# First block's weights split in pieces at lower priority, first query copied by engines, three output pairs begun early

## The chip, the cores and the metric

The kernel runs on one core of one Trainium2 chip. TensorE (PE in the profile) multiplies matrices; VectorE (DVE), ScalarE (ACT) and GpSimd (POOL) work element by element beside it; SyncE (SP) issues most of the DMA transfers, in the order of its own queue. Each engine works through its own list of instructions in order, and the engines wait for one another by semaphores. The metric is the device time of one execution, in microseconds (us): the median of 3 runs of the kernel before is 2264.51 us, the lowest 2261.2 us, the highest 2265.51 us.

## The reference, cut to what matters

```
x, width 1024, 2048 tokens, fp32
h       = rmsnorm(x, g_mix)
u,q,k,v = h @ w_in                       # one combined projection, 4 x 512 columns
ya      = chunked_attention(q, k, v, rel_bias)   # 8 heads of 64; chunk of 64 sees itself and 8 before
ys      = s5_mixer(u, ...)               # diagonal complex state space, scan over tokens, GELU, GLU
x1      = x + concat(rmsnorm(ys), rmsnorm(ya)) @ w_out
out     = rmsnorm(x1 + swiglu(rmsnorm(x1)), g_final)
```

The change touches two places of this: q, k, v and the scores q·k of the first 512 tokens, and `x1` (the output projection with its residual) of the first 512 tokens. Everything is computed to fp32 accuracy.

## The kernel before, in words

**Numbers.** An fp32 value is kept as two parts, high and low, of TensorE's faster type. `split` (L151) makes them: ScalarE copies the high part, VectorE subtracts it from the value. A product is then three matmuls (`mm3`, L145): high by high, high by low, low by high. In the profile such a pair of instructions has line L153, and every matmul has line L76, every transpose L79, so the tile names tell which is which.

**Stages.** The 2048 tokens are four blocks of 512 (`SB`). The first stage makes the norm's factors and u; `att_phase` (L687) makes q, k, v, the scores and the attention, with the state-space part (`ssm_front`, `ssm_back`, whose scan runs on GpSimd) beside it; `mix_phase` (L986) gates the state-space result, norms both halves and multiplies by w_out; the two feed-forward stages follow, and they take by far the most of the time.

**Order.** The code is written against a scheduler: each instruction has a priority, by default its place in the program, and each engine's list is filled by priority among what is ready in the scheduler's own model. `tc.high_priority()` puts the instructions inside ahead of others, and with a negative offset it puts them that many places later than where they stand. TensorE's instructions are kept in program order (`keep_in_program_order`). The lists are fixed when the kernel is built: on the chip an instruction that must wait holds everything behind it on its engine.

**Attention.** There are 128 steps (block, pair of heads, head, 128 queries). In each, `scores` (L840) multiplies a piece of q with k, a VectorE instruction (L866, called ISA in the order, with result `mn`) adds the position bias and takes a minimum, ScalarE takes the exponential; later `transp` (L872) transposes and splits the result, `pv_head` multiplies by v. Projections for later steps are cut into small units and put between the steps (`Unit.advance`, L665).

**Weights of q, k and v.** There are 12 tiles of 128x1024 (0 to 3 q, 4 to 7 k, 8 to 11 v). In the first block `load_ws` (L698) loads each raw tile (two buffers `raw`, shared with x of later blocks) and splits it into one of three buffers `w`, which hold both parts; `keep_w` (L715) stores the split tile to DRAM (`wss`), from where the later blocks load it, 1 MB a tile.

**q and k of a pair.** `qk_unit` (L749) multiplies the tiles for two heads, 64 partitions each. In the first block the result `pf` is first multiplied by the norm's factors (L779: into `xt` for the first pair, `yt` for the others). For each head the high part of q goes to its 64 partitions by ScalarE (L786), the low part by VectorE (L787), and both are copied to the other 64 partitions by two DMAs on SP's queue (L788, L789), because k's high and low parts stand on the two halves of the partitions (L791, L792). For the very first pair the tiles are called `hi0x`, `lo0x` (q of head 0), `hi1x`, `lo1x` (q of head 1), `hi2x`, `lo2x` (k of heads 0 and 1); for later pairs `q2h`, `q2l`, `k`.

**Output projection.** `w_out` (L1118) is a generator for two of the eight row groups of x1, an output pair. It asks for the x tile (`xt`, two buffers), takes a PSUM tile `big` (four buffers, which together are all of PSUM), multiplies the attention half (24 matmuls), pauses, multiplies the state-space half (24 matmuls), and adds x on VectorE (L1133). The tiles `m` hold the normed halves with eight w_out tiles `woh`/`wol`. In the first block the state-space half's norm factors come late: `newton` (L97 to L110) computes them on VectorE in twelve small steps, its result is `no`, `spread` (four transposes, L79) puts them in all partitions, and `rstd2` and `mixed(b, 1)` (L1098, L153) make the tiles `m` for the state-space half. Around that the code writes the pairs by hand:

```
held = [w_out(0, b, 2 * n) for n in range(2)]
next(held[0])                          # pair 0, attention half
spread(...); rstd2(...); mixed(b, 1)
next(held[1])                          # pair 1, attention half
```

After that come the second halves of pairs 0 and 1, the sums for the next block's norms (`ones,sq`), pair 2 as a whole, the spread of those norms, and pair 3.

Of the kernel before, what the change touches and what calls it, by code (L numbers as in the profile page):

```python
# [12 lines left out]
AF = mybir.ActivationFunctionType  # L13
ALU = mybir.AluOpType
# [43 lines left out]
SB_, CB_, GB_ = 5, 5, 10  # L58
DG = 3
DGROUPS = (3, 3, 3, 2), (3, 3, 3)  # L60
LATER = 230
VO, WI, TA = range(3)
LONGS = ((VO, 0),), ((VO, 1),), ((TA, 0), (VO, 2)), ((TA, 1), (VO, 3)), ((TA, 2), (WI, 0)), ((TA, 3), (WI, 1)), ((WI, 2),), ((WI, 3),)
BLOCKS = 1, 2, 3, 0
# [29 lines left out]
def f32(ap):  # L94
    return ap.bitcast(F32)
# [55 lines left out]
def split(k, hi, lo, raw):  # L151
    nc = k.nc
    return nc.scalar.copy(hi, raw), nc.vector.tensor_tensor(lo, raw, f32(hi), op=ALU.subtract)  # L153
# [533 lines left out]
def att_phase(k, ident, S, aw, x0, roots):  # L687

    tc, nc, io, pfs = k.tc, k.nc, k.io, k.pfs
    with ExitStack() as cx:  # L690
        hT, vts, qk, keep = {0: tuple(zip(*x0))}, {}, {}, {}
# [6 lines left out]
        def load_ws(sb, ns):  # L698
            raws = [load_raw(n) for n in ns] if sb == 0 else []
            if raws and ns not in ((0, 4), (8, 10)):  # L700
                yield
            ws = []
            for i, n in enumerate(ns):
                w = k.t(aw, "w", [P, 2, 1024], F32R, bufs=WB)
                if raws:
                    for ins in split(k, w[:, 0], w[:, 1], raws[i][:]):
                        if n in (0, 4):
                            k.tc.keep_in_program_order(ins)
                    keep[n] = w
                else:  # L710
                    nc.sync.dma_start(f32(w[:]), S["ws"][n])
                ws.append((w[:, 0], w[:, 1]))
            return ws
# [34 lines left out]

        def qk_unit(sb, pr):  # L749
            ws = yield from load_ws(sb, (pr, 4 + pr))  # L750
            yield
            hi, lo = hT[sb]
            if (sb, pr) == (0, 0):
                ts = [[k.t(aw, f"{n}{q}x", [P, SB], F32R) for n, q in (("hi", hh), ("lo", hh), (("hi", "lo")[hh], 2))] for hh in range(2)]
            else:
                ts = [(k.t(aa, "q2h", [P, SB], F32R, bufs=3), k.t(aa, "q2l", [P, SB], F32R, bufs=3), k.t(aa, "k2", [P, 2 * SB], F32R, bufs=3)) for _ in range(2)]
            qk[sb, pr] = ts
            if sb > 0:
                for hh in range(2):
                    nc.sync.dma_start(f32(ts[hh][2][:, :SB]), S["k"][(sb - 1) % 2, 2 * pr + hh])  # L760
            both = (sb, pr) == (0, 0)
            pss = []
            for c in range(2):
                if c == 0 or not both:
                    cc = range(2) if both else (c,)
                    pss += [k.t(pfs, "pf", [P, 512]) for _ in cc]
                    for q in range(KT):
                        cs = slice(q * P, (q + 1) * P)
                        for m in cc:
                            wh, wl = ws[m]  # L770
                            mm3(k.ta, pss[m][:], wh[:, cs], wl[:, cs], hi[q], lo[q], q == 0, q == KT - 1)
                            if q == 2:
                                keep_w(4 * m + pr)
                        if q < KT - 1:
                            yield
                ps = pss[c]
                if sb == 0:
                    t = k.t(aa, "yt", [P, SB]) if pr else k.t(aw, "xt", [P, SB], bufs=XB)
                    nc.vector.tensor_tensor(t[:], ps[:], S["rsn"][:, :SB], op=ALU.mult)  # L779
                    ps = t  # L780
                for hh in range(2):
                    q2h, q2l, k2 = ts[hh]
                    a = slice(hh * 64, hh * 64 + 64)
                    o = slice(64 - hh * 64, 128 - hh * 64)
                    if c == 0:
                        nc.scalar.activation(q2h[a, :], ps[a, :], AF.Copy, scale=-0.125)  # L786
                        nc.vector.scalar_tensor_tensor(q2l[a, :], ps[a, :], -0.125, f32(q2h[a, :]), op0=ALU.mult, op1=ALU.subtract)  # L787
                        nc.sync.dma_start(f32(q2h[o, :]), f32(q2h[a, :]))  # L788
                        nc.sync.dma_start(f32(q2l[o, :]), f32(q2l[a, :]))  # L789
                    else:  # L790
                        nc.scalar.copy(k2[a, -SB:], ps[a, :])  # L791
                        nc.vector.tensor_tensor(k2[o, -SB:], ps[a, :], f32(k2[a, -SB:]), op=ALU.subtract)  # L792
                        if sb < NSB - 1:
                            nc.sync.dma_start(S["k"][sb % 2, 2 * pr + hh], f32(k2[:, -SB:]))
                yield
# [190 lines left out]
def mix_phase(k, S, bank):  # L986

    tc, nc, io = k.tc, k.nc, k.io
    te = k.te
    with ExitStack() as cx:  # L990
# [109 lines left out]
        def big():  # L1100
            return k.t(psum, *BIG)
# [16 lines left out]
        def w_out(sb, b, i):  # L1118
            ts = slice(sb * SB, (sb + 1) * SB)
            if i == 0:  # L1120
                b.sa = k.t(k.mf, "sa", [P, SB], bufs=2)
            rows = slice(i * P, (i + 2) * P)
            xt = k.t(wr, "xt", [P, 1024], bufs=2)
            xv = xt[:].rearrange("p (q t) -> p q t", q=2)
            nc.sync.dma_start(xv, io["xt"][rows, ts].rearrange("(q p) t -> p q t", p=P))
            ps = k.t(psum, *BIG)
            for n, c in ((n, c) for m in range(2) for c in range(2) for n in range(4 * m, 4 * m + 4)):
                if n == 4 and c == 0:
                    yield
                fc = slice((i + c) * P, (i + c + 1) * P)  # L1130
                for q in QS[n : n + 1]:
                    mm3(te, ps[:, c * 512 : (c + 1) * 512], W[q][0][:, fc], W[q][1][:, fc], b.m[q][0], b.m[q][1], n == 0, n == 7)
            nc.vector.tensor_tensor(xt[:], xt[:], ps[:], op=ALU.add)  # L1133
            nc.sync.dma_start(S["x1"][rows, ts].rearrange("(q p) t -> p q t", p=P), xv)
            if i == 0:
                nc.scalar.activation(b.sa[:], xt[:, :512], AF.Square)
                nc.scalar.activation(xt[:, 512:], xt[:, 512:], AF.Square)
            else:
                nc.scalar.activation(xt[:], xt[:], AF.Square)
                nc.vector.tensor_tensor(b.sa[:], b.sa[:], xt[:, :512], op=ALU.add)  # L1140
            nc.vector.tensor_tensor(b.sa[:], b.sa[:], xt[:, 512:], op=ALU.add)
            yield
# [22 lines left out]
        b = load(0, True)  # L1165
        load_a(b, 0)
        raws = [load_wo(n, wr, "xt") for n in range(2)]
# [30 lines left out]
        for sb in range(NSB):  # L1198
            if sb:
                b.m = {}  # L1200
                mixed(b, 0)
            if sb == 0:
                held = [w_out(0, b, 2 * n) for n in range(2)]
                next(held[0])
                ps = big()
                spread(k, te, ps[:, :512], b.o[1], 0)
                with tc.high_priority():
                    rstd2(b, 1, ps[:, :512])
                    mixed(b, 1)
                next(held[1])  # L1210
            else:
                mixed(b, 1)
            for n in range(4):
                if n == 0 and 0 < sb < NSB - 1:
                    nxt = next_block(sb + 1)
                if sb or n > 1:
                    for _ in w_out(sb, b, 2 * n):
                        pass
                else:
                    next(held[n])  # L1220
                if n in (0, 1) and xr:
                    next(xr)
                if n in (1, 2) and sb + 1 < NSB:
                    norm(nxt, n - 1)
                for _ in range(PRE0.get((sb, n), 0)):
                    next(pre)
                if (sb, n) == (NSB - 1, 1):
                    rx.close()
                    k.ga1 = tc.alloc_tile_pool(name="ga1", reuse_waits="tile", bufs=1, side="right")
                    k.gr = tc.alloc_tile_pool(name="gr", reuse_waits="tile", bufs=2, side="right")  # L1230
                    wr = cx.enter_context(tc.tile_pool(name="wr2", reuse_waits="tile", bufs=2, side="right"))
                    k.hT = build(k, S, 0, k.ga1, EARLY)
            if sb < NSB - 1:
                xr = rstd_steps(k, te, psum, k.mf, BIG, b.sa[:], D, S["rsn"][:, sb * SB : (sb + 1) * SB])
            if sb == 1:
                pre = pre_steps(k, S, 0, pre_tiles().__next__, True)
            k.last = b.sa[:]
            b = nxt
# [498 lines left out]
```

## Time and profile before

| what | value |
|---|---|
| median of 3 runs (lowest to highest) | 2264.51 us (2261.2 to 2265.51) |
| profiled execution, its own time | 2267.91 us |
| span of the profiled execution | 2266.1 us |
| mean granted TensorE clock | 0.982 |
| TensorE busy | 2165.6 us, 96% |
| VectorE busy | 1542.4 us, 68% |
| ScalarE busy | 1003.3 us, 44% |
| GpSimd busy | 351.2 us, 15% |

The span runs from the first to the last instruction, and the profiled execution's own time is 1.8 us longer. "Busy" counts matmuls with modelled ends, so a busy TensorE is not one that runs at full speed; the granted clock tells the speed. The rows of the timeline give start, duration, engine, line, operation, output<-inputs by the program's names, and in brackets the time for which the engine stood idle before and what it waited for. A row with "x2" groups instructions that follow each other.

### The profile page before, as it was taken

Reading aid. Unit: us, or ns where it says so; the run is one execution under the profiler, and the core shown is the slowest. Engines: PE = TensorE matmul, PEld = TensorE weight load, DVE = VectorE, ACT = ScalarE, POOL = GpSimd, SP = SyncE. Lnnn points to the kernel's source line nnn. Section 1 sums busy time; section 2 is a strip of 40 time slices with the busy share of each in tenths; the row PEclk is TensorE's granted clock in tenths of the full one; section 3 lists DMA queues with packets and bytes.
Section 4 is the critical chain, followed back from the end, with each engine's and each line's share of the span. In section 5 each row is a group of like instructions: output and inputs, shape, how many; then the busy total and the mean of one; then the engine's idle time right before and its main releaser. Section 6 shows DMA issues by size and latency. Waiting matters only on the chain.

```text
span 2266.1 us, 30134 instructions
## 1 busy us (share of the span) xinstructions
PE 2165.6 (96%) x10632; PEld 1825.8 (81%) x10632; DVE 1542.4 (68%) x2695; ACT 1003.3 (44%) x1656; POOL 351.2 (15%) x827
## 2 busy tenths in 40 slices
PE   8988899999997899999999999999999999999997
PEld 6777788898986788778888887888888778888886
DVE  7756666556557756776766668766656477688776
ACT  5445555556557442353333335333333443353322
POOL 2246576656500000000000000000000010000000
PEclk9999999999998899999999999999999999999999
DMA  8878876666552435754556457645433395465652
GB/s 276 254 244 261 268 233 207 192 190 205 187 168 100 138 109 188 251 168 144 180 176 209 162 198 269 199 163 190 140 97 112 102 385 182 167 227 181 216 183 75
DMA packets 194903, 430.41 MB, mean 190 GB/s; under 512 B 19904, under 2 KB 38384, under 8 KB 187648
## 3 DMA queue, kind: packets, MB, share of 16 engines
q1 hardware_dynamic: 187104, 403.58, 53.8%
q0 software_dynamic: 7648, 24.92, 3.6%
q8 instruction: 83, 1.36, 0.2%
q14 instruction: 68, 0.56, 0.1%
HBM read 288.95 MB, written 131.10 MB: 185 GB/s over the span
## 4 chain that ended last, share of the span: by engine, by line
PE 78%; DMA 7%; DVE 6%; ACT 3%; issue 2%; SPq 0%; DVEq 0%; ACTq 0%
PE X L76 20%; PE ps L76 17%; PE Y L76 10%; PE pf L76 10%; PE big L76 6%; PE W L76 5%; PE pj L76 4%; PE pt L79 2%; PE sc L76 2%; DMA acc<-x 2%; DMA lo<-hc 1%; DMA xt<-in_xt 1%; DVE lo L153 1%; DMA hc<-gh 1%; DVE ptl L885 1%
## 5 line engine op out<-in xcount | busy, mean ns | idle before, releaser
L76 PE MATMUL X<-hi,c 128*128 128x512 f32 x1408 | 450.8, 391 | 7.4 <-DVE c L153 5.1
L76 PE MATMUL ps<-hd,hd 128*128 128x512 f32 (+1 forms) x1968 | 429.6, 380 | 3.0 <-DVE hd L153 2.0
L76 PEld LDWEIGHTS ps<-hd,hd 128*128 128x128 f32 x1968 | 357.5, 189 | 73.6 <-DVE hd L153 2.7
L76 PEld LDWEIGHTS X<-hi,c 128*128 128x128 f32 x1408 | 265.1, 188 | 64.1 <-DVE c L153 6.0
L76 PE MATMUL X<-lo,c 128*128 128x512 f32 x704 | 274.6, 390 | 0.0
L153 ACT CAST hd<-hd 128x1536 fp32r<-128x1536 f32 (+1 forms) x106 | 147.5, 1394 | 232.5 <-DMA hd<-hq 170.9
L76 PE MATMUL Y<-hi,c 128*128 128x512 f32 x704 | 226.0, 392 | 3.8 <-DVE c L153 2.3
L153 DVE TENSOR_TENSOR hd<-hd 128x1536 fp32r<-128x1536 f32 (+1 forms) x106 | 174.1, 1644 | 36.2 <-ACT hd L153 35.8
L153 DVE TENSOR_TENSOR c<-S,c 128x512 fp32r<-128x512 f32 x176 | 121.0, 688 | 103.6 <-ACT c L153 103.3
L1516 POOL DMA_DIRECT2D hd<-hq x7 | 5.3, 755 | 1173.2 <-PE X L76 1161.5
L1408 ACT COPY u<-X 128x512 f32<-128x512 f32 x132 | 77.4, 587 | 199.9 <-PE X L76 199.9
L153 ACT CAST c<-S 128x512 fp32r<-128x512 f32 x176 | 109.5, 622 | 122.5 <-PE Y L76 63.8
L76 PE MATMUL big<-m,woh 128*128 128x512 f32 x512 | 162.6, 399 | 0.0
L76 PEld LDWEIGHTS Y<-hi,c 128*128 128x128 f32 x704 | 133.3, 189 | 32.4 <-DVE c L153 2.8
L1550 DVE TENSOR_TENSOR acc<-acc,ps 128x512 f32<-128x512 f32 x196 | 130.2, 682 | 41.6 <-PE ps L76 41.3
L76 PEld LDWEIGHTS X<-lo,c 128*128 128x128 f32 x704 | 132.6, 188 | 27.4
L76 PE MATMUL pf<-hi,w 128*128 128x512 f32 x416 | 149.1, 410 | 0.0
L153 ACT CAST c<-raw 128x512 fp32r<-128x512 f32 x132 | 82.2, 622 | 149.1 <-PE Y L76 69.1
L76 PE MATMUL Y<-lo,c 128*128 128x512 f32 x352 | 137.7, 391 | 0.0
L885 DVE TENSOR_TENSOR ptl<-pt,pth 128x640 fp32r<-128x640 f32 (+3 forms) x152 | 98.3, 647 | 56.1 <-ACT pth L884 54.7
L869 ACT ACTIVATE s<-s,mn 128x640 f32<-128x640 f32 (+4 forms) x128 | 98.0, 765 | 64.1 <-DVE mn L866 58.1
L884 ACT CAST pth<-pt 128x640 fp32r<-128x640 f32 (+3 forms) x152 | 83.8, 551 | 85.6 <-PE pt L79 80.9
(448 smaller groups left out, 4274.1 us busy)
## 6 DMA issues: line engine op xcount, KB each, us to landing
w<-wss SPq DMA_DIRECT2D x36, 1024.0 KB, 6.2
hq<-g SPq DMA_DIRECT2D x140, 256.0 KB, 2.1
hd<-hq SPq DMA_DIRECT2D x35, 768.0 KB, 4.4
hd<-wc SPq DMA_DIRECT2D x35, 768.0 KB, 6.0
raw<-in_w_gate SPq DMA_DIRECT2D x44, 512.0 KB, 3.7
raw<-in_w_up SPq DMA_DIRECT2D x44, 512.0 KB, 4.2
wc<-px SPq DMA_DIRECT2D x66, 256.0 KB, 3.1
wss<-w SPq DMA_DIRECT2D x12, 1024.0 KB, 6.5
```

The costliest lines, as they stand in the source:

```text
L76: return self.tc.keep_in_program_order(self.tc.nc.tensor.matmul(*a, **b))
L79: return self.tc.keep_in_program_order(self.tc.nc.tensor.transpose(*a, **b))
L153: return nc.scalar.copy(hi, raw), nc.vector.tensor_tensor(lo, raw, f32(hi), op=ALU.subtract)
L869: nc.scalar.activation(s[:, :nk], s[:, :nk], AF.Exp, bias=mn[:], scale=-1.0, accum_out=sums[sb, pr][:, hh, qp : qp + 1])
L884: nc.scalar.copy(pth[:, a:b, qp, :], pt[:, a:b, :])
L885: nc.vector.tensor_tensor(ptl[:, a:b, qp, :], pt[:, a:b, :], f32(pth[:, a:b, qp, :]), op=ALU.subtract)
L1408: nc.scalar.copy(u[:], ps[:])
L1516: (nc.gpsimd if aside else nc.sync).dma_start(f32(lo), src.rearrange("g p c -> p g c"))
L1550: V.tensor_tensor(a, a, ps[:], op=ALU.add)
```

## The change

There are three parts.

1. `load_ws`: in the first block every weight tile but those of the first pair (0 and 4) is split in two pieces of 512 columns instead of one of 1024, and the four instructions are put 100 places later in priority (`WAY`).
2. `qk_unit`: for head 0 of the first pair, ScalarE and VectorE write q's two parts to both halves of the partitions; its two DMAs are left out. Head 1 and all later pairs keep theirs.
3. `mix_phase`: three output pairs are held. The attention halves of pairs 0 and 1 stand ahead of the spread, that of pair 2 behind it; the second half of pair 2 stands where all of pair 2 stood.

```diff
-LATER = 230
+LATER, WAY = 230, 100
...
                 w = k.t(aw, "w", [P, 2, 1024], F32R, bufs=WB)
-                if raws:
+                if raws and n in (0, 4):
                     for ins in split(k, w[:, 0], w[:, 1], raws[i][:]):
-                        if n in (0, 4):
-                            k.tc.keep_in_program_order(ins)
+                        k.tc.keep_in_program_order(ins)
+                    keep[n] = w
+                elif raws:
+                    with tc.high_priority(offset=-WAY):
+                        for h in range(2):
+                            hs = slice(h * 512, h * 512 + 512)
+                            split(k, w[:, 0, hs], w[:, 1, hs], raws[i][:, hs])
                     keep[n] = w
...
                     if c == 0:
-                        nc.scalar.activation(q2h[a, :], ps[a, :], AF.Copy, scale=-0.125)
-                        nc.vector.scalar_tensor_tensor(q2l[a, :], ps[a, :], -0.125, f32(q2h[a, :]), op0=ALU.mult, op1=ALU.subtract)
-                        nc.sync.dma_start(f32(q2h[o, :]), f32(q2h[a, :]))
-                        nc.sync.dma_start(f32(q2l[o, :]), f32(q2l[a, :]))
+                        ways = (a, o) if both and hh == 0 else (a,)
+                        for w in ways:
+                            nc.scalar.activation(q2h[w, :], ps[a, :], AF.Copy, scale=-0.125)
+                            nc.vector.scalar_tensor_tensor(q2l[w, :], ps[a, :], -0.125, f32(q2h[a, :]), op0=ALU.mult, op1=ALU.subtract)
+                        if len(ways) == 1:
+                            nc.sync.dma_start(f32(q2h[o, :]), f32(q2h[a, :]))
+                            nc.sync.dma_start(f32(q2l[o, :]), f32(q2l[a, :]))
...
-                held = [w_out(0, b, 2 * n) for n in range(2)]
+                held = [w_out(0, b, 2 * n) for n in range(3)]
                 next(held[0])
+                next(held[1])
                 ps = big()
                 spread(k, te, ps[:, :512], b.o[1], 0)
                 with tc.high_priority():
                     rstd2(b, 1, ps[:, :512])
                     mixed(b, 1)
-                next(held[1])
+                next(held[2])
...
-                if sb or n > 1:
+                if sb or n > 2:
```

The change also moves instructions, since the lists are made anew. Three places follow. In the order each row has the line, the operation, output<-inputs with the tiles' numbers, and the shape; new lines of code push the line numbers up by 5 to 9.

VectorE's list ahead of the first scores, of the kernel before and then of the changed one; `xt` is q or k after the norm's factors, `w` a weight tile, `lo0x` and `hi2x` the parts of q and k that the first scores read, ISA the first work on the scores.

```order
L779 TENSOR_TENSOR xt_1513<-pf_1390,rsn_93 128x512
L779 TENSOR_TENSOR xt_1523<-pf_1391,rsn_93 128x512
L153 TENSOR_TENSOR w_1538<-raw_1533,w_1538 128x1024
L787 SCALAR_TENSOR_TENSOR lo0x_1385<-xt_1513,hi0x_1384 64x512
L787 SCALAR_TENSOR_TENSOR lo1x_1388<-xt_1513,hi1x_1387 64x512
L792 TENSOR_TENSOR hi2x_1386<-xt_1523,hi2x_1386 64x512
L792 TENSOR_TENSOR lo2x_1389<-xt_1523,lo2x_1389 64x512
L153 TENSOR_TENSOR w_1607<-raw_1603,w_1607 128x1024
L866 ISA s_1565,mn_1566<-sc_1562,nba_107 128x128
```

```order
L784 TENSOR_TENSOR xt_1513<-pf_1390,rsn_93 128x512
L153 TENSOR_TENSOR w_1540<-raw_1533,w_1540 128x512
L784 TENSOR_TENSOR xt_1523<-pf_1391,rsn_93 128x512
L794 SCALAR_TENSOR_TENSOR lo0x_1385<-xt_1513,hi0x_1384 64x512 x2
L794 SCALAR_TENSOR_TENSOR lo1x_1388<-xt_1513,hi1x_1387 64x512
L800 TENSOR_TENSOR hi2x_1386<-xt_1523,hi2x_1386 64x512
L800 TENSOR_TENSOR lo2x_1389<-xt_1523,lo2x_1389 64x512
L153 TENSOR_TENSOR w_1540<-raw_1533,w_1540 128x512
L874 ISA s_1569,mn_1570<-sc_1566,nba_107 128x128
L874 ISA mn_1570 128x1
L153 TENSOR_TENSOR w_1611<-raw_1607,w_1611 128x512 x2
```

One weight tile is now in two pieces around q and k, a second one stands behind the first ISA, and `lo0x` is written twice.

SP's list near the first block's last pair, before and then after; `y<-U` stores a state-space result, `w<-wss` loads a split weight tile for the second block, `U` and `Bst` are loaded for the next state-space group.

```order
L654 DMA y_65<-U_1708 128x1024
L788 DMA q2h_2507<-q2h_2507 64x512
...
L789 DMA q2l_2511<-q2l_2511 64x512
L711 DMA w_2618<-wss_74 128x2048
L726 DMA xt_2659<-in_xt 128x512
...
L566 DMA U_2665<-u_64 128x1024
L566 DMA Bst_2667<-bsts_70 128x512
```

```order
L716 DMA w_2638<-wss_74 128x2048
L796 DMA q2h_2527<-q2h_2527 64x512
...
L797 DMA q2l_2531<-q2l_2531 64x512
L654 DMA y_65<-U_1716 128x1024
L731 DMA xt_2679<-in_xt 128x512
...
L566 DMA U_2685<-u_64 128x1024
L566 DMA Bst_2687<-bsts_70 128x512
```

The weight load and the store of y have changed places around the copies of q; the load of U, which goes into the buffer that y is stored from, has the store closer ahead of it.

TensorE's list at the output projection of the first block, before and then after; one `big` is the PSUM tile of an output pair (8539 and 8559 are pair 0), `ident,no` is the spread.

```order
L76 MATMUL big_8539<-m_1836_8478,wol_1844_8494 128x512
L79 MATMUL big_8564<-ident_80,no_8423 128x128 x4
L76 MATMUL big_8587<-m_1833_8469,woh_1837_8481 128x512 x2
...
L76 MATMUL big_8587<-m_1836_8478,wol_1844_8494 128x512
L76 MATMUL big_8539<-m_1867_8573,woh_1845_8497 128x512 x2
```

```order
L76 MATMUL big_8559<-m_1836_8498,wol_1844_8514 128x512
L76 MATMUL big_8586<-m_1833_8489,woh_1837_8501 128x512 x2
...
L76 MATMUL big_8586<-m_1836_8498,wol_1844_8514 128x512
L79 MATMUL big_8611<-ident_80,no_8443 128x128 x4
L76 MATMUL big_8634<-m_1833_8489,woh_1837_8501 128x512 x2
...
L76 MATMUL big_8634<-m_1836_8498,wol_1844_8514 128x512
L76 MATMUL big_8559<-m_1869_8620,woh_1845_8517 128x512 x2
```

The attention half of a second pair (24 matmuls) now stands ahead of the spread, and that of a third pair between the spread and the second half of pair 0.

## The prediction

> **What bounds the kernel now.** I read the page's totals first, then its chain, then TensorE's waits in the two stretches that the change touches: 120 to 300 us (first block) and 700 to 970 us (output projection).
>
> ```profile
> span 2266.1 us, 30134 instructions
> PE 2165.6 (96%) x10632; PEld 1825.8 (81%) x10632; DVE 1542.4 (68%) x2695; ACT 1003.3 (44%) x1656; POOL 351.2 (15%) x827
> PE 78%; DMA 7%; DVE 6%; ACT 3%; issue 2%; SPq 0%; DVEq 0%; ACTq 0%
> ...
> PE sc L76 <- DMA hi0x<-hi0x: 6.3, 1, 6.3
> PE sc L76 <- DVE mn L866: 5.8, 1, 5.8
> PE pj L76 <- DMA Bst<-bsts: 4.0, 1, 4.0
> ...
> PE big L79 <- DVE no L110: 7.9, 1, 7.9
> ```
>
> TensorE carries the kernel (96% busy, 78% of the chain). So a change is worth what it takes from TensorE's idle time, or adds to it, and a microsecond gained early is kept if no later wait on something slower swallows it. The four waits above are the places: the first scores (6.3 us, on a DMA that part 2 removes), the scores behind weight splitting (5.8), a load in the first block (4.0), the spread in the output projection (7.9, which part 3 fills).
>
> **First scores (part 2, with part 1).**
>
> ```profile
> 131.09 1.37 DVE L779 TENSOR_TENSOR xt<-pf,rsn 128x512 f32<-128x512 f32 x2 [5.52 <-PE pf L76]
> 132.37 1.22 DVE L153 TENSOR_TENSOR w<-raw,w 128x1024 fp32r<-128x1024 f32 x1
> 132.69 0.50 SPq L788 DMA_DIRECT2D hi0x<-hi0x  x1
> 133.50 0.78 DVE L787 SCALAR_TENSOR_TENSOR lo0x<-xt,hi0x 64x512 fp32r<-64x512 f32 x1
> 134.31 0.48 SPq L789 DMA_DIRECT2D lo0x<-lo0x  x1
> 134.31 0.69 DVE L787 SCALAR_TENSOR_TENSOR lo1x<-xt,hi1x 64x512 fp32r<-64x512 f32 x1
> 135.03 0.70 DVE L792 TENSOR_TENSOR hi2x<-xt,hi2x 64x512 fp32r<-64x512 f32 x1
> 138.05 0.44 PE L76 MATMUL sc<-hi2x,hi0x 128*128 128x128 f32 x1 [6.32 <-DMA hi0x<-hi0x]
> ...
> L153 DVE TENSOR_TENSOR c<-S,c 128x512 fp32r<-128x512 f32 x176 | 121.0, 688 | 103.6 <-ACT c L153 103.3
> L153 ACT CAST c<-S 128x512 fp32r<-128x512 f32 x176 | 109.5, 622 | 122.5 <-PE Y L76 63.8
> ...
> L153 DVE TENSOR_TENSOR w<-raw,w 128x1024 fp32r<-128x1024 f32 x9 | 10.9, 1224 | 2.1 <-ACT w L153 2.1
> L153 ACT CAST w<-raw 128x1024 fp32r<-128x1024 f32 x9 | 9.3, 1043 | 1.6 <-PE pf L76 1.5
> ```
>
> The reader sees VectorE done with k (`hi2x`) at 135.73, and TensorE still waiting for the copies of q until 138.05. Without head 0's two DMAs the scores wait for VectorE's list, which the order gives: from 131.09 two `xt` (1.37), one weight piece between them (0.69, by the row of the same operation at 512 columns), `lo0x` twice and `lo1x` (start to start 0.81 and 0.72 in the rows, so 0.81 + 0.72 + 0.72) and `hi2x` (0.70). That ends at 136.1, and ScalarE's two `hi0x` run beside it. Gain: 138.05 - 136.1 = **2.0 us**; bounds 2.3 (`hi2x` done at 135.73 as now) and 0 (`hi1x` or SP's queue still late for the next step). Head 1's scores come four steps later, so its DMAs are covered; were they not, the old 2 us would be back.
>
> **Weights in pieces (part 1).** Ten tiles. A tile costs ScalarE 2 x 0.622 - 1.043 = 0.20 us more and VectorE 2 x 0.688 - 1.224 = 0.15 more: 2.0 and 1.5 us of engine time in all, beside TensorE (VectorE is 68% busy). Most of it costs nothing while the engine has idle time ahead of the scores. One place has none:
>
> ```profile
> 192.02 2.36 DVE L153 TENSOR_TENSOR w<-raw,w 128x1024 fp32r<-128x1024 f32 x2 [0.27 <-ACT w L153]
> 194.74 0.55 PE L76 MATMUL sc<-k,q2h 128*128 128x256 f32 x1 [5.84 <-DVE mn L866]
> ```
>
> Two whole tiles stand ahead of the minimum that the scores wait for. In the new order both tiles, now four pieces, still stand ahead of it, so I leave this wait as it is (0.3 either way). Elsewhere the new order puts the fourth pair's q ahead of the last transposes' low parts (near 230 us), about 1.1 us late for the next product, and near 214 us lets `ptl` pass between weight pieces, about 0.5 us early; both are counted in rows of 0.3 to 0.7 us like those above. Net **+0.6**.
>
> **SP's queue (moved by the new order).**
>
> ```profile
> 228.42 0.33 SPq L654 DMA_DIRECT2D y<-U  x1
> 234.10 0.54 SPq L711 DMA_DIRECT2D w<-wss  x1
> 236.61 0.71 SPq L566 DMA_DIRECT2D U<-u  x1
> 237.37 0.45 SPq L566 DMA_DIRECT2D Bst<-bsts  x1
> 245.65 3.35 PE L76 MATMUL pj<-U,Bst 128*128 128x256 f32 x8 [4.04 <-DMA Bst<-bsts]
> ...
> 228.00:236.00 8.00, 7.87 (x39) 6.19 (x38) 6.36 (x17) 5.47 (x15) 0.00 (x0) 1.00 0.58 158
> 236.00:252.00 16.00, 9.76 (x43) 7.67 (x41) 10.23 (x21) 9.67 (x23) 1.12 (x3) 0.89 1.00 354
> ...
> w<-wss SPq DMA_DIRECT2D x7, 1024.0 KB, 7.0
> U<-u SPq DMA_DIRECT2D x2, 512.0 KB, 7.1
> ```
>
> The windows' last two columns are the DMA engines' share and GB/s: half idle before 236 us, full after it. The 1 MB weight load moves from 234.1 to about 229, into the idle part, and `y`, 512 KB like the U that it is read from, moves from 228.4 to about 234. So the full stretch has 0.5 MB less, at 354 GB/s 1.4 us, and `Bst`'s landing (8.1 us or so after issue) is **1.4 us** earlier, beside the 1.4 us by which the queue as a whole runs ahead (2.0 - 0.6). Against it: U's load now waits for `y`'s landing, with SP's queue behind it. Bounds: TensorE reaches this wait at 240.2 instead of 241.6, so no more than 4.0 can go; and if `y` takes as long as the load of U did (issued 236.61, 8.3 to landing), issued at 232.7 it lands at 241.0, U's issue is 4.4 late and the landing of `Bst` 3.6 late. I take the 1.4, since by bytes the queue empties sooner. From 228 us on the first block stands at 2.0 - 0.6 + 1.4 = 2.8 us early.
>
> **Output projection (part 3).**
>
> ```profile
> 737.51 0.39 PE L76 MATMUL big<-m,wol 128*128 128x512 f32 x1
> 745.83 1.09 PE L79 MATMUL big<-ident,no 128*128 128x128 f32 x4 [7.93 <-DVE no L110]
> 746.57 1.20 PE L76 MATMUL big<-m,woh 128*128 128x512 f32 x2
> 750.40 0.63 PE L76 MATMUL big<-m,woh 128*128 128x512 f32 x2
> 759.54 1.22 DVE L1133 TENSOR_TENSOR xt<-xt,big 128x1024 f32<-128x1024 f32 x1
> 770.99 0.28 DVE L110 SCALAR_TENSOR_TENSOR no<-nf,ny 128x4 f32<-128x4 f32 x2
> ...
> 975.00 5.44 PE X L76 x24
> ```
>
> TensorE stands 7.93 us until VectorE's Newton steps give `no`. The attention half of pair 1 is 24 matmuls on tiles that pair 0 has just used, so nothing new has to be ready: 5.44 us, by the chain's row of 24. It fits into the 7.93, and 2.5 us of waiting are left. After the spread, pair 2's half takes the place of pair 1's, covering the same `rstd2` and `mixed`. Pair 2 then needs only 24 matmuls after the norm sums, which begin at 766.84; 5.44 and the slow start end near 774. By then `no` of the norms is there (770.99 + 0.28), and pair 0's PSUM buffer, which the sums take, was free at 760.8. Pair 2's `xt` load is issued behind pair 1's store, about 2 us later than now, and is needed only for the add at 774. Gain **5.4 us**; bounds 4.0 (`no` later by the 1.4 us of VectorE's moved sums) and 7.2 (below). What follows runs on TensorE without a long wait, so I carry it to the end.
>
> **The clock.** After the 7.93 us, the nine matmuls from 746.57 to 750.40 take 3.83 us; at 0.227 each (5.44 / 24) they would take 2.04. So the slow restart costs 1.8 us. Does it also follow a wait of 2.5 us? Two rows differ:
>
> ```profile
> 238.77 0.30 PE L76 MATMUL sc<-k,q2h 128*128 128x128 f32 x1 [2.20 <-issue]
> 965.57 1.22 PE L76 MATMUL Y<-hi,c 128*128 128x512 f32 x2 [2.33 <-DVE c L153]
> ```
>
> After 2.20 us the matmul ran fast, after 2.33 (with a 1.68 wait before) it ran at half rate, 0.61 each. I take the slow restart as kept, since 2.5 is on the side of the second. [...]
>
> **Sum.** First scores -2.0, reordering +0.6, SP's queue -1.4, output projection -5.4, clock 0: **-8.2 us**. The profiled execution took 2267.9, so 2259.7 in its terms. It is 3.4 above the median of 2264.5, which gives **2256.3**.
>
> **Rivals.**
>
> *The clock stays up.* For it: the 2.20 row; against: the 2.33 row. Another 1.8 off: 2264.5 - 10.0 = 2254.5.
>
> *The first block gives its gain back.* `Bst` lands 3.6 late, as worked out, instead of 2.8 early: 2264.5 + 3.6 - 5.4 = 2262.7, a change of 0.1%. For it: 512 KB loads in the full stretch take 8 us; against: `y` alone need not.
>
> *Slower: the weights come too late.* Pieces 100 places later in priority may be ready only when TensorE already wants them. There are five later projections in the first block (pairs 1 to 3, two of v), each on two tiles; a tile that is late holds TensorE for its four instructions, 2 x (0.62 + 0.69) = 2.6 us, two tiles for 5.2. At the middle, 3.9 each, five give 19.5: 2264.5 - 8.2 + 19.5 = 2275.8. It decides from 2.5 us each on, (8.2 + 4.5) / 5. For it: the 5.84 us wait shows that weight splitting already reaches TensorE once; against: in the new order the pieces still stand ahead of the work of the steps that need them.
>
> **How the numbers follow.** My forecast 0.45, clock up 0.25, gain given back 0.20, weights late 0.10. A change of 0.2%, 4.5 us, is about what a measurement of this kernel can tell from none; so faster is below 2260.0 and slower above 2269.0: 0.70, 0.20, 0.10. Low end: clock up and the whole `Bst` wait gone (2.6 more): 2251.9, with the first scores' bound 0.3 more, 2251.6. High end: gain given back with 4.0 instead of 5.4 in the output projection, 2264.1. I give 2251.6 to 2264.1, outside which lie the late weights and little more.
>
> **What would show it.** First scores waiting for `hi2x` or `lo0x` on VectorE, near 136. The `Bst` wait near 243 and under 4 us. Before the spread a wait of about 2.5 us on `no` with 24 matmuls ahead of it; matmuls behind it at 0.43 (clock down) or 0.23 (up). Pair 2's add near 771 (774 less the 2.8). I am wrong if waits of `pf` on `w` L153 appear in the first block, if `Bst`'s wait is over 6 us, or if a wait on `xt` or on VectorE behind pair 2 takes the 5.4 us back.

## The result and the profile after

The changed kernel takes 2253.69 us (median of 6 runs, 2247.43 to 2255.98), the kernel before 2264.52 (median of 6). The ratio is 0.9948, with a 95% interval of 0.9932 to 0.9963: faster by 0.5%, about 11 us. The forecast was 2256.3, within 2251.6 to 2264.1.

The profile after is of the fastest of the six executions, 2247.43 us. It lies 20 us below the profile before, so nearly half of what the two traces differ by isn't the change. The first lines of its page, and the clock of both (the view of the cores, before and then after):

```profile
span 2245.7 us, 30154 instructions
...
PE 2155.6 (96%) x10632; PEld 1817.4 (81%) x10632; DVE 1543.3 (69%) x2706; ACT 1004.6 (45%) x1667; POOL 352.4 (16%) x827
```

```profile
core 0: 2266.1 us, clock 0.982
```

```profile
core 0: 2245.7 us, clock 0.988
```

TensorE's waits after, first 120 to 300 us, then 700 to 970:

```profile
PE pt L79 <- DVE ptl L893: 6.3, 6, 3.1
PE sc L76 <- DVE mn L874: 5.7, 1, 5.7
PE sc L76 <- DVE hi2x L800: 4.2, 1, 4.2
PE pj L76 <- DMA Bst<-bsts: 2.6, 1, 2.6
...
PE big L79 <- DVE no L110: 2.5, 1, 2.5
```

The four waits of the prediction are 4.2 (was 6.3, and now on VectorE's `hi2x` instead of a DMA), 5.7 (5.8), 2.6 (4.0) and 2.5 (7.9). The spread and what follows it, in the timeline after:

```profile
739.55 0.62 PE L79 MATMUL big<-ident,no 128*128 128x128 f32 x4 [2.50 <-DVE no L110]
739.92 0.71 PE L76 MATMUL big<-m,woh 128*128 128x512 f32 x2
740.47 0.40 PE L76 MATMUL big<-m,wol 128*128 128x512 f32 x1
740.71 0.62 PE L76 MATMUL big<-m,woh 128*128 128x512 f32 x2
```

Three matmuls of a group now take 0.79 us (739.92 to 740.71) where they took 1.28 (3.83 for nine): the clock stayed up behind this wait, granted at 1.00 from 741 to 813 us, where the trace before has 0.50 from 740.0 to 750.2.

TensorE runs the same number of matmuls in both kernels, in an order that differs only at the output projection. So each instruction's start can be set against that of the same place in the trace before, and the difference shows where time goes. The tables below give it in us, worked out so from the traces. The first counts from 128.7 us (before the changed part; up to there executions differ by up to 3.7 either way), at five places of the trace before; the second counts from 733.3 us.

| kernel | 139, first scores | 195, head 3's scores | 236 | 249, behind `Bst` | 302 |
|---|---|---|---|---|---|
| changed kernel | -2.13 | -2.12 | -3.98 | -5.14 | -4.92 |
| parts 1 and 2 | -2.14 | -1.75 | -3.34 | -4.32 | -4.04 |
| part 2 alone | -1.49 | -0.13 | -0.79 | -0.58 | -0.63 |
| part 1 alone | +0.36 | -0.42 | -0.73 | -4.09 | -3.37 |
| part 3 alone | +0.24 | -0.33 | -1.13 | -1.25 | -1.41 |

The last row has no edit in this stretch: it shows what one execution differs from another by itself, 1.4 us here. Four of the kernels below (parts 1 and 2, and the three that move 12 or 6 matmuls of an output pair) have the same lists as the changed kernel up to 300 us. They and the changed kernel stand at -3.34 to -4.27 at 236 us, at -4.21 to -5.43 at 249 and at -2.72 to -5.19 at 302. So a difference of up to 2.5 us at 302 can be the execution's alone.

| kernel | wait for `no` | half clock behind it | 827, behind the norm sums |
|---|---|---|---|
| changed kernel | 2.5 | no | -8.82 |
| part 3 alone | 2.4 | no | -8.88 |
| changed kernel, head 3's minimum first | 2.6 | no, but behind the norm sums | -7.05 |
| changed kernel, 12 matmuls of pair 1 behind the spread | 5.2 | yes | -3.68 |
| changed kernel, y's store ahead | 2.5 | yes | -5.54 |
| parts 1 and 3 | 2.5 | yes | -5.57 |

### The profile page after: what moved, and what is told of

Same layout as the page of the kernel before. It is cut to its first block, busy times and chain, and to the rows that moved or that the text cites. A ratio compares the mean times of both kernels' runs of the same rounds, so it can differ in the third digit from the quotient of the medians.

```text
span 2245.7 us, 30154 instructions
## 1 busy us (share of the span) xinstructions
PE 2155.6 (96%) x10632; PEld 1817.4 (81%) x10632; DVE 1543.3 (69%) x2706; ACT 1004.6 (45%) x1667; POOL 352.4 (16%) x827
## 3 DMA queue, kind: packets, MB, share of 16 engines
q8 instruction: 83, 1.36, 0.2%
## 4 chain that ended last, share of the span: by engine, by line
PE 81%; DVE 7%; DMA 4%; ACT 3%; issue 2%; SPq 0%; DVEq 0%; ACTq 0%
PE X L76 20%; PE ps L76 19%; PE Y L76 10%; PE pf L76 10%; PE big L76 7%; PE W L76 5%; PE pj L76 4%; PE pt L79 2%; PE sc L76 2%; DMA lo<-hc 1%; DMA xt<-in_xt 1%; DVE ptl L893 1%; DMA x<-xt 0%; DVE s L874 0%; DVE lo L153 0%
```

## The experiments

All times are medians; each ratio is to runs of the kernel before on the same chip, and "us faster" goes by the ratio. The experiments ran on three chips, on which the kernel before took 2262.60, 2262.76 and 2264.15 us, so times are compared by their ratios. Each trace is of one execution.

### The three parts apart

```diff
 # part 3 alone: the kernel before with
-                held = [w_out(0, b, 2 * n) for n in range(2)]
+                held = [w_out(0, b, 2 * n) for n in range(3)]
                 next(held[0])
+                next(held[1])
...
-                next(held[1])
+                next(held[2])
...
-                if sb or n > 1:
+                if sb or n > 2:
```

> The kernel before with part 3 alone (three output pairs held). Theory one, the parts are independent and the clock stays up after a short wait: the wait for the result of the Newton steps is 2.5 us instead of 7.9, the matmuls behind it stand 0.23 us apart, no granted clock of 0.5 is recorded there, and the median is near 2264.5 - 5.4 - 1.8 = 2257. Rival, the full clock in the changed kernel's profile was the luck of one execution: 0.43 apart and 2259. Rival, the gain needs the first block's earlier work: the wait stays over 5 us and the time within 2 of before.

2255.21 us, ratio 0.9971 (0.9957 to 0.9985): 6.6 us faster. The wait for `no` is 2.4 us and no stretch at half clock follows. So the part works alone, and in this execution the clock stayed up.

```diff
 # parts 1 and 2: the changed kernel with
-                held = [w_out(0, b, 2 * n) for n in range(3)]
+                held = [w_out(0, b, 2 * n) for n in range(2)]
                 next(held[0])
-                next(held[1])
...
-                next(held[2])
+                next(held[1])
...
-                if sb or n > 2:
+                if sb or n > 1:
```

> The changed kernel without part 3 (two pairs held, as before), so parts 1 and 2 together. Theory: the first scores start 2.1 us earlier, the rest of the first block gains 2 to 3 more by 300 us, the wait for the Newton result is 7.9 us as before with a slow restart behind it; median near 2260.5. Rival, the first block's gain is luck of one execution and is only the 2.1: 2262.4.

2258.43 us, ratio 0.9978 (0.9966 to 0.9989): 5.0 us faster. With part 3's 6.6 that makes 11.6, what the whole change shows (11.8 by its ratio): the two places add up, within intervals of some 3 us either way.

```diff
 # part 2 alone: the kernel before with
+                        ways = (a, o) if both and hh == 0 else (a,)
+                        for w in ways:
+                            nc.scalar.activation(q2h[w, :], ps[a, :], AF.Copy, scale=-0.125)
+                            nc.vector.scalar_tensor_tensor(q2l[w, :], ps[a, :], -0.125, f32(q2h[a, :]), op0=ALU.mult, op1=ALU.subtract)
+                        if len(ways) == 1:
...
```

> The kernel before with part 2 alone (head 0's query written to both halves by the engines, no DMAs for it). Theory: the first scores wait for VectorE's last piece of k and start near 136 instead of 138, 2 us, and nothing else moves; the wait for Bst stays near 4 us; median near 2262.4. Rival, the whole weight tile that still stands ahead on VectorE (1.22 instead of 0.69) takes some of it: 1.5 us.

2264.86 us, ratio 1.0008 (0.9995 to 1.0021): no gain to be measured. The first scores start 1.5 us earlier, as the rival with the whole tile said, but by 195 us that is gone, in the trace to 0.1 us. The timeline of part 2 alone shows where, beside the same place before:

```profile
162.17 1.40 DVE L153 TENSOR_TENSOR w<-raw,w 128x1024 fp32r<-128x1024 f32 x1 [0.66 <-ACT w L153]
163.50 0.55 DVE L888 TENSOR_TENSOR ptl<-pt,pth 128x384 fp32r<-128x384 f32 x1
164.10 0.45 PE L76 MATMUL pj<-ptl,v 128*128 128x384 f32 x1 [1.08 <-DVE ptl L888]
```

```profile
162.61 1.23 DVE L153 TENSOR_TENSOR w<-raw,w 128x1024 fp32r<-128x1024 f32 x1 [0.32 <-ACT w L153]
...
167.29 0.56 DVE L885 TENSOR_TENSOR ptl<-pt,pth 128x384 fp32r<-128x384 f32 x1 [0.55 <-ACT pth L884]
167.91 0.44 PE L76 MATMUL pj<-ptl,v 128*128 128x384 f32 x1 [0.15 <-DVE ptl L885]
```

In the kernel before, the split of the weight tile is done 3.4 us before this `ptl` begins. In part 2's list, made anew, it stands directly ahead of `ptl`, which TensorE needs next, and holds VectorE for 1.40 us in one piece. TensorE then waits 1.08 us where it waited 0.15.

```diff
 # part 1 alone: the kernel before with
+                elif raws:
+                    with tc.high_priority(offset=-WAY):
+                        for h in range(2):
+                            hs = slice(h * 512, h * 512 + 512)
+                            split(k, w[:, 0, hs], w[:, 1, hs], raws[i][:, hs])
...
```

> The kernel before with part 1 alone (weight tiles in pieces of 512 columns at lower priority). Theory: the first scores wait for the DMA of the query as before, near 138; the gains after 195 us (earlier pieces for a projection near 215, a shorter wait for Bst) are of this part: 1 to 2.5 us by 300 us; median near 2263. Rival, they come from being earlier by part 2: 0 +- 0.5 by 300 us and 2264.5. Rival, weights late: waits of the projections on weight splitting, slower by up to 5.

2260.41 us, ratio 0.9992 (0.9978 to 1.0006): 1.8 us, not clear of none. Its trace has the shorter waits near 215 and at `Bst`, so these belong to part 1. (At `Bst` TensorE waits only 0.5 us, in part because half clock ahead of it, with matmuls 0.43 us apart near 244 us instead of 0.23, made it 1.5 us late.) By 302 us it has gained 3.4, more than expected. No wait on late weights appears.

### What in part 1 matters, and part 2 beside it

```diff
-                        for h in range(2):
-                            hs = slice(h * 512, h * 512 + 512)
-                            split(k, w[:, 0, hs], w[:, 1, hs], raws[i][:, hs])
+                        split(k, w[:, 0], w[:, 1], raws[i][:])
```

> The changed kernel, but the weight tiles are split whole again, at the lower priority. Theory, the pieces are what matters in part 1 and the priority is not: with whole tiles the query's early start is lost again where a whole tile stands ahead of the transposes' low parts near 165 us (a wait of about 1 us there), and the 1 us near 215 goes; first block 1 us early by 200 us instead of 2 or more; median 2256. Rival, the lower priority is what matters: waits as in the changed kernel, 2253.

2257.56 us, ratio 0.9969 (0.9958 to 0.9979). First scores at -1.49 as with part 2 alone, -0.65 by 195 us, with a wait of 1.1 us on `ptl`; -1.95 by 302. The gain of part 2 is lost at the same place, so whole tiles are the cause there and the lower priority doesn't prevent it:

```profile
163.16 1.42 DVE L153 TENSOR_TENSOR w<-raw,w 128x1024 fp32r<-128x1024 f32 x1 [0.66 <-ACT w L153]
...
165.10 0.45 PE L76 MATMUL pj<-ptl,v 128*128 128x384 f32 x1 [1.10 <-DVE ptl L891]
```

```diff
-LATER, WAY = 230, 100
+LATER, WAY = 230, 0
```

> The changed kernel with the priority offset 0 instead of 100, pieces kept. Theory, the priority does nothing: the waits of the first block up to 250 us are those of the changed kernel within 0.3 us, median 2253.5. Rival, it matters: a longer wait of the scores near 190 us or a wait of 1 us near 165, 2256.

2257.72 us, ratio 0.9969 (0.9958 to 0.9981). Three waits of the first block stay as they are (5.8 near 190, 4.2 for the first scores, 2.2 for `Bst`), but the theory fails, and already near 170 us, as the rival said. This run first, then the changed kernel:

```profile
165.51 1.57 DVE L153 TENSOR_TENSOR w<-raw,w 128x512 fp32r<-128x512 f32 x2
167.01 0.54 DVE L874 CUSTOM_DVE_ANT_0 s<-sc,nbb 128x384 f32<-128x384 f32 x1
...
169.94 0.44 PE L79 MATMUL pt<-ident,s 128*128 128x128 f32 x2 [1.51 <-DVE ptl L893]
...
216.09 0.44 PE L79 MATMUL pt<-ident,s 128*128 128x128 f32 x2 [0.65 <-DVE ptl L893]
...
279.68 0.42 PE L76 MATMUL sc<-k,q2h 128*128 128x320 f32 x1 [1.65 <-DVE mn L874]
...
283.11 0.69 PE L76 MATMUL pj<-ptl,v 128*128 128x384 f32 x1 [1.36 <-DVE ptl L893]
```

```profile
164.62 0.69 DVE L153 TENSOR_TENSOR w<-raw,w 128x512 fp32r<-128x512 f32 x1
165.22 0.55 DVE L874 CUSTOM_DVE_ANT_0 s<-sc,nbb 128x384 f32<-128x384 f32 x1
165.70 0.94 DVE L153 TENSOR_TENSOR w<-raw,w 128x512 fp32r<-128x512 f32 x1
...
168.16 0.44 PE L79 MATMUL pt<-ident,s 128*128 128x128 f32 x2 [0.64 <-DVE ptl L893]
...
283.83 1.26 PE L79 MATMUL pt<-ident,s 128*128 128x128 f32 x5 [3.11 <-DVE ptl L893]
```

At the higher priority both pieces of a tile stand ahead of the scores' minimum (L874), and TensorE then waits 0.9 us longer; at the lower one the second piece stands behind it. Near 215 us another 0.6 us of waiting stays that the changed kernel doesn't have. So the priority isn't idle: it decides which work the pieces let pass. By 249 us this run is 2.6 us behind the changed kernel; how much of that the granted clock makes isn't shown. The new waits near 281 us add little, since the changed kernel's wait of 3.11 us behind them is gone here: by 302 us it has gained 2.0 us where the changed kernel has 4.9. The interval overlaps that of the changed kernel, so how much of this is in the median stays open.

```diff
-                        ways = (a, o) if both and hh == 0 else (a,)
...
+                        nc.sync.dma_start(f32(q2h[o, :]), f32(q2h[a, :]))
+                        nc.sync.dma_start(f32(q2l[o, :]), f32(q2l[a, :]))
```

> The changed kernel without part 2 (head 0's query copied by DMAs again), so parts 1 and 3. Theory, part 2 is worth its 2.1 us only beside the pieces, which keep it: median 2 above the changed kernel, 2256, first scores on the DMA at a wait of 6.3 instead of 4.2. Rival, part 2 is worth nothing in any company, as alone: 2253.7.

2257.88 us, ratio 0.9967 (0.9954 to 0.9980), some 4 us above the changed kernel by the ratios, though their intervals overlap. The first scores wait 6.2 us for the DMA again. At 236 us it stands at -1.55, and the five kernels with both parts and the same lists at -3.34 to -4.27: beside the pieces the early query keeps its gain to there, alone it has lost it by 195. At 302 us it stands at -3.33, inside their range, so what is kept to the end isn't shown by the traces.

### The load of U behind y's store

```diff
-    nc.sync.dma_start(S["y"]...)
+    with k.tc.high_priority(offset=300 if b == 0 else 0):
+        nc.sync.dma_start(S["y"]...)
```

> The changed kernel, but SP's list has the store of y ahead of the copies of the query and the weight load behind them, as in the kernel before. Theory, the bytes ahead of Bst decide its landing: the wait for it is 1.4 us longer again, about 4 us. Rival, the load of U that waits for the store's landing decides: the wait is shorter, under 2 us. Rival, neither: 2.6 +- 0.5. In the median too small to be seen.

2253.25 us, ratio 0.9959 (0.9942 to 0.9975). SP's queue and the matmul on `Bst`, with the store ahead and then in the changed kernel:

```profile
223.98 0.33 SPq L655 DMA_DIRECT2D y<-U  x1
...
228.06 1.71 SPq L717 DMA_DIRECT2D w<-wss  x1
...
232.05 0.50 SPq L566 DMA_DIRECT2D Bst<-bsts  x1
...
240.86 3.34 PE L76 MATMUL pj<-U,Bst 128*128 128x256 f32 x8 [1.84 <-DMA Bst<-bsts]
```

```profile
223.47 0.33 SPq L716 DMA_DIRECT2D w<-wss  x1
...
227.86 0.58 SPq L654 DMA_DIRECT2D y<-U  x1
...
232.95 0.34 SPq L566 DMA_DIRECT2D U<-u  x1
233.33 0.43 SPq L566 DMA_DIRECT2D Bst<-bsts  x1
...
239.59 3.64 PE L76 MATMUL pj<-U,Bst 128*128 128x256 f32 x8 [2.61 <-DMA Bst<-bsts]
```

The wait is under 2 us, as the rival said, but its length misleads. In this execution TensorE ran at half clock ahead of it (matmuls 0.43 us apart near 237 us, and 0.23 at the same place in the changed kernel; granted clock 0.76 from 230.5 to 245 us, and 0.88 there) and came late. From issue to use `Bst` takes 8.8 us with the store ahead and 6.3 in the changed kernel, though it is issued later there. All profiles in which TensorE waits for `Bst` divide this way: 8.3 to 8.9 us in the five with the store ahead, 6.2 to 7.1 in the eight with the weight load ahead. (With whole weight tiles the list has the store ahead, so this order too came with the pieces.) On the other side, U is issued in the changed kernel at 232.95, when y has landed (227.86 and 5.07 us), with `Bst` behind it. So the load is faster and the load of U does wait for y. What is left of the two can't be told from none: between 225 and 249 us the changed kernel gains 1.0 us on the trace before and this one 0.4, but the other four with the changed kernel's lists gain 0.2 to 1.3. That the bytes ahead of `Bst` make the difference is the reading that I had forecast; no run changes the bytes alone.

### The scores behind weight splitting

```diff
 # VectorE's part of tiles 9 and 11, and head 3's first minimum, kept in program order
...
-Unit(gen, n + 1, C[c], C[c + 1], 4, light=LIGHT, mid=2)
+Unit(gen, n + 1, C[c], C[c + 1], 4, light=LIGHT, mid=0 if c == 4 else 2)
...
```

> The changed kernel, but in the first block the weight tiles 9 and 11 are split later, and VectorE's list has the first minimum of head 3 ahead of them. Theory: the 5.7 us wait of the scores near 190 us is VectorE splitting two weight tiles ahead of that minimum, 2.5 us of it, so the wait is 3.2 and the time 2.5 us shorter unless v's projection then waits for its weights: 2251. Rival, the wait is made by the chain of k (q and k of the pair, 2.6 us) and the splits only fill it: the wait stays over 5 us. Rival, the weights then come too late for v: a wait of 2 to 3 us there, 2254.

2252.14 us, ratio 0.9953 (0.9937 to 0.9969): the same as the changed kernel.

```profile
188.93 0.55 PE L77 MATMUL sc<-k,q2h 128*128 128x256 f32 x1 [3.67 <-DVE mn L877]
...
193.44 0.58 PE L77 MATMUL pf<-w,hi 128*128 128x256 f32 x1 [2.68 <-DVE w L154]
```

The wait falls from 5.7 to 3.7 us and 2.7 come back right behind it, where v's projection waits for the same weights, as the rival with the late weights said. VectorE has that work to do before TensorE can go on, in whichever order.

### The clock and the length of the wait

```diff
 # half of pair 1's first 24 matmuls moved behind the spread, by one more yield
+MID = (2,)
...
-                if n == 4 and c == 0:
+                if (n == 4 and c == 0) or (n == 0 and c == 1 and sb == 0 and i in MID):
                     yield
...
+                next(held[1])
                 next(held[2])
```

> The changed kernel, but only 12 of pair 1's 24 matmuls stand ahead of the spread, the other 12 behind it. TensorE then waits about 5.2 us for the Newton result instead of 2.5. Theory, the clock falls only when TensorE is idle for a whole window of about 3.4 us (the length of the stretches at 0.5 in the records): a 5.2 us wait holds a whole window in about half of the executions, so 2.7 us slower than the changed kernel, or 4.5 with the clock down: median 2257. Rival, any wait over 2 us lets the clock fall: always down behind it. Rival, only the wait of 7.9 does: always up.

2255.08 us, ratio 0.9963 (0.9949 to 0.9978). The wait is 5.2 us and the clock is down behind it, as after 7.9; it holds a whole idle window here, so this run doesn't tell the theory from its first rival. The windows below are cut where the records of the clock change, 3.41 us each: first this kernel, then the changed one (wait 2.50), then the one with y's store ahead (wait 2.53). The columns are the stretch, its length, the busy time of TensorE (matmuls, weight loads), VectorE, ScalarE and GpSimd, the granted clock, the DMA share and GB/s.

```profile
735.15:738.57 3.42, 0.00 (x0) 0.00 (x0) 3.42 (x10) 1.66 (x3) 0.00 (x0) 1.00 0.44 122
738.57:741.98 3.41, 2.42 (x8) 2.17 (x9) 2.71 (x6) 2.42 (x4) 0.00 (x0) 0.50 1.04 311
```

```profile
734.51:737.92 3.41, 2.54 (x12) 1.76 (x10) 3.41 (x11) 2.30 (x5) 0.00 (x0) 1.00 0.49 166
737.92:741.34 3.42, 1.79 (x10) 1.61 (x11) 3.18 (x8) 2.40 (x4) 0.00 (x0) 1.00 1.01 292
741.34:744.75 3.41, 3.41 (x16) 2.82 (x16) 3.41 (x7) 3.11 (x6) 0.00 (x0) 1.00 0.97 294
```

```profile
739.64:743.06 3.42, 0.89 (x6) 0.46 (x5) 3.39 (x9) 1.64 (x3) 0.00 (x0) 1.00 0.61 155
743.06:746.47 3.41, 3.41 (x11) 2.82 (x10) 3.20 (x6) 2.97 (x6) 0.00 (x0) 0.50 1.09 339
```

The same wait of 2.5 us fell across two windows in the changed kernel (0.87 and 1.63 us idle) and the clock stayed up; with y's store ahead it fell into one (2.53 idle) and the next ran at half. The theory of the whole idle window is out by this. Of the seven profiles with a wait of about 2.5 us (2.34 to 2.61), four kept the clock and three did not.

```diff
 # 12 of pair 2's matmuls ahead of the spread, 12 behind it
+MID = (4,)
...
-                if n == 4 and c == 0:
+                if (n == 4 and c == 0) or (n == 0 and c == 1 and sb == 0 and i in MID):
                     yield
...
                 next(held[1])
+                next(held[2])
                 ps = big()
```

> The changed kernel, but 12 matmuls of pair 2 also stand ahead of the spread, 12 behind it. Theory: the 2.5 us wait is filled (2.7 us of work), and 2.7 us are left to cover the norm of the state-space half behind it, whose first tile comes about 3.5 us after the spread and the others 0.65 apart: a new wait of 0.5 to 1.5 us on the tiles m; net 1 to 2 us faster than the changed kernel, 2252. Rival, the norm of the state-space half needs all the cover of 24 matmuls: the wait moves there whole, no gain, 2254.

2251.80 us, ratio 0.9952 (0.9935 to 0.9968). No wait for `no` is left; the new one is on `m`:

```profile
748.96 0.50 PE L77 MATMUL big<-m,woh 128*128 128x512 f32 x1 [1.42 <-DVE m L154]
```

That is in the range expected, and 1.1 us of the 2.5 is kept: too little to be told in the median.

```diff
 # 6 ahead, 18 behind: the same with an earlier yield
-                if n == 4 and c == 0:
+                if (n == 4 and c == 0) or (n == 2 and c == 0 and sb == 0 and i in MID):
                     yield
...
```

> The changed kernel, but 6 of pair 2's matmuls stand ahead of the spread, 18 behind it. Theory, the clock falls when a window of 3.4 us holds about 1.9 us of idle time: the wait for the Newton result is 1.1 us and the new one on the tiles m under 0.3, so the clock stays up in every execution and 1.2 us of waiting goes: median 2252, no granted clock of 0.5 between 725 and 755 us. Rival, the wait on m is as long as with 12 ahead (1.4): 2253.5. Rival, the clock falls for another reason: 0.5 recorded there.

2250.17 us, ratio 0.9936 (0.9916 to 0.9956), the lowest of all, though its interval overlaps that of the changed kernel. The two waits are

```profile
738.73 0.62 PE L80 MATMUL big<-ident,no 128*128 128x128 f32 x4 [0.96 <-DVE no L111]
744.06 0.50 PE L77 MATMUL big<-m,woh 128*128 128x512 f32 x1 [0.35 <-DVE m L154]
```

1.3 us instead of 2.5, and no half clock between 725 and 755 us. No window holds more than 0.97 us of these waits, and by the counts in the last section no window with so little lost the clock unless it held norm sums. So I expect it to stay up here in every execution, an estimate from these counts; one was traced. In that one it fell behind the norm sums, from 757.72 us on.

## Why the prediction was right

The time came out 2.6 us below the forecast and inside the range, but 0.8 below the rival with the clock up (2254.5) and so nearer to that one; in the changed kernel's trace the matmuls behind the wait are 0.23 us apart, which was that rival's sign. The forecast was a gain of 8.2 us, and 10.8 were measured by the medians, 11.8 by the ratio. The places and what was waited for were right; the sizes were not all. By its steps:

- **First scores, -2.0.** Right: -2.13 in the changed kernel, and the wait is on `hi2x`. What I didn't see is that this gain needs part 1. I used the order of the whole change, in which the pieces let `ptl` pass; alone, part 2 starts only 1.49 earlier and loses 1.1 of that to one whole weight tile 30 us later.
- **Weights in pieces; the 5.8 us wait stays.** Right: 5.7, and no wait on late weights. That rival is out.
- **Reordering, +0.6.** The wrong sign. Between 195 and 236 us the changed kernel gains 1.9 us. 1.2 of it, near 200 us, is where the stretch of half clock ended (TensorE was busy for 5.93 us of it in the trace before, for 3.21 in the changed kernel's), which another execution needn't have (with y's store ahead it is 0.2); near 215 a wait of 1.0 us on `ptl` goes, where I had counted 0.5; and the 1.1 us loss near 230 is 0.2 to 0.7 in the traces with that order.
- **SP's queue, -1.4.** -1.2 in the trace, but how much of it is due to the order isn't shown: the run with the store ahead lies inside the spread of the kernels without that edit. The load itself is faster, as forecast (6.2 to 7.1 us from issue to use, against 8.3 to 8.9). The rival that gives the first block's gain back is out: U waits for y, and TensorE's wait for `Bst` is 2.6 us all the same, not over 6.
- **Output projection, -5.4.** Right to a few hundredths: the wait goes from 7.93 to 2.50, with 24 matmuls ahead of it and nothing late behind; where the clock fell as before, the place gains 5.5 to 5.8.
- **Clock, 0.** The step that is off in kind. I asked whether 2.5 us keeps the clock and chose no; in the runs it went by how the wait fell on the windows (2.53 us in one of them, or 0.87 and 1.63 in two), and three of seven profiles lost it. Between them the place differs by 3.3 us (-8.8 against -5.5), which also holds whether the norm sums 20 us later took the clock. Where only these took it, the place stands at -7.05: the restart itself is then worth 1.5, near the 1.8 forecast. The term should have been a mean, about 1 us of gain by four of seven.

The sum of the terms was 8.2; the parts measured 5.0 (2.5 to 7.7) and 6.6 (3.4 to 9.7). The first block's 2.8 and the output projection's 5.4 lie inside these intervals, on the low side. The terms for the clock and for the reordering are too low by the traces. The first block's own wanderings between executions, up to 2.5 us with the same lists, are of the size of what is missing, so no single term can be charged with the rest. That the number stayed inside the range in spite of these misses owes something to luck.

## What to carry to other kernels

A wait for a small chain on another engine is best filled with independent work that is already in the program; what it pays is the length of that work, and here the trace of before gave it to a tenth of a microsecond, but for what the clock does behind it. An early start is kept only if nothing indivisible on another engine stands in the way later: cutting long off-path instructions into pieces, and putting them behind the short work that is waited for, can be what makes another edit pay. When single executions differ by more than the change, compare the same instructions' starts place by place, and try the parts apart.

## What the runs showed of the hardware

In each of the 14 profiles of this study the stretches at a granted clock of 0.5 start whole multiples of 3.41 us apart. I counted TensorE's idle time in each window of that grid that ran at full clock between 20 and 2200 us. With 2.0 us idle or more, the next window was at half in 112 of 112 cases; with 1.6 to 2.0, in 24 of 47; with less, in 24 of 8527. Of these last 24, 20 hold norm sums, whose matmuls write a single column each (128x1 in the timeline); in the trace before, one of them has 0.26 us of idle time and is followed by 0.50 from 767.28 us on. The other four stood idle for 1.36 to 1.44 us. Why the clock fell behind the norm sums isn't shown. In the rows above, 2.53 us of idle time in one window were enough (at 739.64), and 0.87 and 1.63 us in two that follow each other were not (at 734.51). By these counts I'd expect a wait of about 1.6 to 4 us in this kernel to take the clock or not by how it falls on the grid, and one of over 4 us to take it, since one window then holds 2 us of it (an estimate from the counts). So two executions can differ by some 3 us at one such place: -8.82 and -5.54 at the output projection, where TensorE's list is the same.
